# Combined feed-forward weights kept in DRAM after the first token block, and the down projection's differences on VectorE

## The chip, the cores and the metric

The kernel runs on one core of one Trainium2 chip. The metric is the device time of one execution in microseconds (us). The kernel before has a median of 3090.89 us over 3 runs (3089.71 to 3095.99).

## The reference

One layer of a hybrid decoder for 2048 prompt tokens and 32 sample tokens, all in float32. A first half (a gated linear recurrence beside dilated attention) makes `mix`, and then:

```
h  = x + mix @ w_o
hn = rmsnorm(h)
u  = hn @ w_gate                      # 1024 -> 2816
c  = conv_b + sum_j conv_w[j] * u[t - 2 + j]
h  = h + (silu(c) * (hn @ w_up)) @ w_down
h  = h + sigmoid(rmsnorm(h) @ w_ple_gate) * (p @ w_ple_proj)
y  = rmsnorm(h)
```

The change lies in the middle part: the gate, up and down projections.

## The kernel before

Every product of float32 numbers is made of three TensorE passes (`mm3`, L138): each operand is split into a rounded high half and the rest, and high times high, high times rest and rest times high are summed in PSUM. The halves of a weight tile of 128x512 are made by `split_to` (L175): ScalarE copies the raw tile into the high half (L176), VectorE subtracts it from the raw tile to get the rest (L177).

The program has three parts in time. Up to about 1230 us come the input projections, the recurrence and the attention. While the first of the input phases runs, a generator (`down_weights`, L182) makes the down projection's weights on the side: for each of 11 pairs of rows of blocks it loads four quarters, combines and splits them, and stores seven results to a DRAM tile `wd_d`; the loop at L1507 takes two steps of it per step of the phase. Then comes the `trunk` (L936): the tokens are cut into three blocks of 696, 696 and 688, and all blocks pass first through the output projection (`out_block`), then through the feed-forward part (`ffn_block`, L1217), then through the last part (`embed_block`). The feed-forward part of block 0 runs from about 1430 to 1870 us, of block 1 to about 2350 us, of block 2 to about 2810 us.

In the feed-forward part a step `f` (11 in each block) makes 256 of the 2816 columns. A 2x2 product costs seven instead of eight block products (Strassen's scheme in Winograd's form). It needs seven weight operands, numbered 1 to 7 and used in the order 1, 5, 6, 7, 4, 2, 3: numbers 1, 2 and 4 are quarters as they stand in the input; 5, 6, 7 and 3 are sums and differences of quarters. `quarters` (L1135) makes the seven for a gate or an up projection: four loads of 256 KB on SyncE's queue (SP, L942) into the pool of `raw` tiles (7 buffers), then `factors` (L160) with four operations on GpSimd (POOL):

- L164 adds two quarters, when both have landed;
- L166 and L168 subtract;
- L172 overwrites the second scratch tile, so that it waits until VectorE has split what stood there (operand 6).

Each operand is split into a `w` tile, of which there are 6. Before the change this is done anew in each of the three blocks: 66 times in all.

After the up projection, `pair` (L1304) makes the operands of the down projection from the two result tiles `a` and `e`: four differences on POOL (L1315, L1316, L1318, L1319) into two tiles `u`, then ScalarE's copy (L1306) and VectorE's rest (L1307). The `u` tiles are shared with the gate's results of the next step.

The down projection of two steps makes a group (`downs`, L1183). Its seven products are laid between the gate and up products as fourteen halves, one for each entry of `todo`. Its weights are fetched from `wd_d` by DMAs that POOL issues (L1193, 512 KB each, two for each of the seven), into a pool `dw` of 5 buffers: `fetch(x + 2)` is issued when product x starts. POOL works through its instructions in order, and so do SP's queue and ScalarE; the order on each engine is fixed when the program is built, by a scheduler that simulates the program.

Of the kernel before, what the change touches and what calls it, by code (L numbers as in the profile page):

```python
# [11 lines left out]
F32 = mybir.dt.float32  # L12
F32R = mybir.dt.float32r
# [27 lines left out]
USE = (1, 5, 6, 7, 4, 2, 3)  # L41
DOWN_USE = (1, 6, 7, 4, 5, 3, 2)
PAIRS = NF // 2
# [4 lines left out]
def hymba_step_kernel(ctx: ExitStack, tc: tile.TileContext, I: dict, O: dict):  # L48
    nc = tc.nc
    V, A, G, PE, SP = nc.vector, nc.scalar, nc.gpsimd, nc.tensor, nc.sync  # L50

    const = ctx.enter_context(tc.tile_pool(name="const", bufs=1))
    dram = ctx.enter_context(tc.tile_pool(name="scratch", bufs=1, space=DRAM))
# [32 lines left out]
    mix_d = dram.tile([128, NK, NTOK], F32, name="mix_d")  # L86

    wd_d = [dram.tile([7, 128, 2, 512], F32R, name=f"wd{p}_d") for p in range(PAIRS)]
    h_d, hn_d, h2_d = [dram.tile([128, NK, NTOK], F32, name=n) for n in ("h_d", "hn_d", "h2_d")]

    def f32(ap):
        return ap.bitcast(F32)
# [45 lines left out]
    def mm3(ps, wh, wl, xh, xl, first, last, read=False):  # L138

        PE.matmul(ps, lhsT=wh, rhs=xh, start=first, stop=False, skip_group_check=read)  # L140
        PE.matmul(ps, lhsT=wh, rhs=xl, start=False, stop=False, skip_group_check=read)  # L141
        PE.matmul(ps, lhsT=wl, rhs=xh, start=False, stop=last, skip_group_check=read)  # L142
# [14 lines left out]
                lo, hi = 292 * r, 292 * (r + 1)  # L157
                A.dma_start(O[dst][b, lo:hi], I[src][b, lo + 4:hi + 4])

    def factors(a11, a12, a21, a22, tile_, split):  # L160

        yield 1, split(a11)
        s1, s2 = tile_(), tile_()
        G.tensor_add(s1, a21, a22)  # L164
        yield 5, split(s1)
        G.tensor_sub(s2, s1, a11)  # L166
        yield 6, split(s2)
        G.tensor_sub(a21, a11, a21)  # L168
        yield 7, split(a21)
        yield 4, split(a22)  # L170
        yield 2, split(a12)
        G.tensor_sub(s2, a12, s2)  # L172
        yield 3, split(s2)

    def split_to(w, raw):  # L175
        A.copy(w[:, 0], raw)  # L176
        V.tensor_sub(w[:, 1], raw, f32(w[:, 0]))  # L177
        return w
# [3 lines left out]
    def down_weights(pool):  # L182

        tile_ = lambda: pool.tile([128, 512], F32, name="draw", bufs=8)
        for p in range(PAIRS):
            a = [tile_() for _ in range(4)]
            with tc.issue_after(recent[0].ins):
                for x, (i, j) in zip(a, itertools.product(range(2), repeat=2)):
                    SP.dma_start(x, I["w_down"][2 * p + j][:, 512 * i:512 * i + 512])
            for n, w in factors(*a, tile_, lambda raw: split_to(pool.tile([128, 2, 512], F32R, name="dw", bufs=3), raw)):  # L190
                SP.dma_start(f32(wd_d[p][n - 1]), f32(w))
                yield

# [742 lines left out]
    def trunk(cst, rp, ev, sm, tw, hp, sh, wp, dw, pmm, pdn):  # L936
        def raw_tile():
            return rp.tile([128, 512], F32, name="raw")

        def load(src):  # L940
            raw = raw_tile()
            SP.dma_start(raw, src)  # L942
            return raw
# [188 lines left out]
                pair(2, 3, i, xb[i])  # L1132
            yield

        def quarters(src, f):  # L1135

            a = [load(src[f + i][:, 512 * j:512 * j + 512]) for i in range(2) for j in range(2)]
            return dict(factors(*a, raw_tile, split))

        def strassen(w, X, H, put, after, before=lambda n: None):  # L1140

            def product(ps, n, first=True, last=True):
                before(n)
                for k in range(4):
                    kw = slice(128 * k, 128 * k + 128)
                    mm3(ps[:, :H], w[n][:, 0, kw], w[n][:, 1, kw], *X[n][k], first and k == 0, last and k == 3, n not in (2,))
                after(n)

            def copied():
                t = sh.tile([128, 348], F32, name="s")[:, :H]  # L1150
                A.copy(t, pa[:, :H])  # L1151
                return t

            pa, pb, pc = [pmm.tile([128, 512], F32, name="mm") for _ in range(3)]
            product(pa, 1)
            s1 = copied()
            product(pb, 5)
            product(pa, 6, False)
            s2 = copied()
            product(pa, 7, False)  # L1160
            s3 = copied()
            put(1, 1, lambda o, v: V.tensor_add(o, v(pb), v(s3)))
            product(pa, 4, False)
            put(1, 0, lambda o, v: A.copy(o, v(pa)))
            product(pc, 2)
            put(0, 0, lambda o, v: V.tensor_add(o, v(pc), v(s1)))
            product(pb, 3, False)
            put(0, 1, lambda o, v: V.tensor_add(o, v(pb), v(s2)))
# [48 lines left out]
        def ffn_block(b, s, ahead):  # L1217
            t0, T, npr = TRUNK[b]
            H = T // 2
# [4 lines left out]
            for f in range(0, NF, 2):  # L1224
# [36 lines left out]
                def to_u(i, j, put):  # L1261
# [3 lines left out]
                    if n < H:  # L1265
                        put(u[:, npr + 2:npr + 50].rearrange("p (b t) -> p b t", t=6)[:, :, 2:6],
                            lambda t: t[:, n:H].rearrange("p (b t) -> p b t", t=4))

                strassen(quarters(I["w_gate"], f), s.X, H, to_u, after_gate, before)
                gms = []  # L1270
                for i in range(2):
                    u = us[i]
# [19 lines left out]
                def to_gm(i, j, put):  # L1292
# [2 lines left out]
                    cs = slice(H * j, H * j + H)  # L1295
                    V.tensor_mul(gms[i][:, cs], gms[i][:, cs], t)

                strassen(quarters(I["w_up"], f), s.X, H, to_gm, after_up)

                one, two = slice(0, H), slice(H, T)  # L1300
                (a, t), (e, u) = [(g, ev.tile([128, 706], F32, name="u")[:, :T]) for g in gms]
# [2 lines left out]
                def pair(n1, n2, x, n=0):  # L1304
                    hi, lo = wide(T, F32R), wide(T, F32R)
                    copy_after(A.copy(hi, x), n)  # L1306
# [8 lines left out]
                G.tensor_sub(t[:, one], a[:, two], a[:, one])  # L1315
                G.tensor_sub(t[:, two], e[:, two], t[:, one])  # L1316
                pair(5, 6, t, 2 if f < NF - 4 else 0)
                G.tensor_sub(u[:, one], e[:, two], a[:, two])  # L1318
                G.tensor_sub(u[:, two], e[:, one], t[:, two])  # L1319
# [125 lines left out]
        class Block:  # L1445
# [31 lines left out]
    pool = pools(in_st)  # L1477
# [28 lines left out]

    for i, _ in enumerate(in_phase(0, *args, plv, po)):  # L1507
        if i > 8:
            step(down, 2)
    step(down, 1000)  # L1510
    down_st.close()
    pool = pools(hgrn_st, side="right")
    hc, ld, wk, sp = pool("h_c", 1), pool("h_l", 2), pool("h_w", 2), pool("h_s", 2)
    S = []
    for h in range(4):
        s = sp.tile([128, 128], F32, name=f"S{h}")
# [15 lines left out]
    pool = pools(attn_st)  # L1532
# [27 lines left out]
    with ExitStack() as st:  # L1560
        pool = pools(st)
        cp = pool("ffn_c", 1)
        cst = {}
        cst["taps"] = cp.tile([128, NF, 4], F32, name="taps")
        SP.dma_start(cst["taps"], I["taps"])
        cst["conv_s"] = cp.tile([128, NF, 8, 2], F32, name="conv_s")
        SP.dma_start(cst["conv_s"], I["conv_s"])
        cst["halo"] = cp.tile([128, NF, 2], F32, name="halo")
        G.memset(cst["halo"], 0.0)

        tr, tp, dw, ts, th, te, tw, hp = [pool(n, k) for n, k in (
            ("tr", 7), ("tp", 6), ("dw", 5), ("ts", 1), ("th", 6), ("te", 2), ("tw", 44), ("thh", 8))]
# [142 lines left out]
```

## Time and profile before

| | |
|---|---|
| median of 3 runs | 3090.89 us |
| the profiled execution's own time | 3090.4 us |
| its span, first to last instruction | 3088.6 us |
| PE (TensorE matmul) busy | 2952.6 us, 96% |
| DVE (VectorE) busy | 2322.6 us, 75% |
| ACT (ScalarE) busy | 1304.4 us, 42% |
| POOL (GpSimd) busy | 1150.1 us, 37% |
| mean granted TensorE clock | 0.978 |

A group line of the profile has: line, engine, operation, output<-input, shapes, count | busy us, mean ns of one | idle time of the engine before them and what ended it. A line of the waits says which engine and line waited for which, the total in us, how often, and the longest. "L176" is line 176 of the kernel before.

### The profile page before, as it was taken

To read this page: it belongs to the slowest core of one execution; us is meant where nothing else is said; L and a number is where in the kernel's file an instruction comes from. 1 tells how busy PE (TensorE), PEld (TensorE's weight loads), DVE (VectorE), ACT (ScalarE), POOL (GpSimd) and SP (SyncE) were. 2 spreads that over 40 slices of the span, in tenths; PEclk is the share of its full clock that TensorE was granted. 3 is DMA by queue.
4 is the path that set the end of the run, shared out by engine and by line. 5 is a ranking of instruction groups with operands and counts; after the bars stand their busy time and mean duration, and the time that the engine had idled before them with its cause. 6 is when DMAs were issued, how large, how long until landed. Compare 5 with 4: busy or idle time off the path is not lost.

```text
span 3088.6 us, 51939 instructions
## 1 busy us (share of the span) xinstructions
PE 2952.6 (96%) x18639; PEld 2736.8 (89%) x18639; DVE 2322.6 (75%) x4715; ACT 1304.4 (42%) x2824; POOL 1150.1 (37%) x1066
## 2 busy tenths in 40 slices
PE   8999999999889899999999998999999999999998
PEld 8988799987676566998999998999998999999997
DVE  6657757867587687568878678867789878887677
ACT  4332422222266565334444443444444544444443
POOL 1443222222233352003554453545453554543331
PEclk9999999999989999999999999999999999999998
DMA  5899433333438986774556666465667566667453
GB/s 184 321 346 324 144 98 106 110 125 97 134 93 244 261 260 206 252 256 153 176 195 211 206 219 222 160 206 193 211 196 239 185 209 212 205 203 250 139 173 128
DMA packets 296898, 606.38 MB, mean 196 GB/s; under 512 B 42881, under 2 KB 110593, under 8 KB 294849
## 3 DMA queue, kind: packets, MB, share of 16 engines
q1 hardware_dynamic: 259792, 414.96, 41.6%
q0 software_dynamic: 33264, 121.13, 12.3%
q10 hardware_dynamic: 3584, 66.98, 5.9%
q8 instruction: 147, 2.41, 0.3%
q14 instruction: 111, 0.90, 0.1%
HBM read 479.09 MB, written 190.85 MB: 217 GB/s over the span
## 4 chain that ended last, share of the span: by engine, by line
PE 43%; DVE 8%; issue 3%; DMA 3%; POOL 2%; ACT 1%; DVEq 0%; ACTq 0%; POOLq 0%; SPq 0%
PE mm L140 14%; PE mm L142 14%; PE mm L141 14%; DMA w<-wd_d 2%; DVE w L177 2%; DVE h L1209 1%; DVE w L1285 1%; DVE w L1286 1%; POOL raw L164 1%; DVE w L1352 1%; POOL raw L168 0%; ACT w L176 0%; DMA raw<-in_w_up_dram 0%; POOL raw L166 0%; DVE w L1019 0%
## 5 line engine op out<-in xcount | busy, mean ns | idle before, releaser
L141 PE MATMUL mm<-w 128*128 128x348 f32 (+3 forms) x3636 | 1173.7, 323 | 2.2 <-DVE w L1352 1.7
L140 PE MATMUL mm<-w 128*128 128x348 f32 (+3 forms) x3508 | 1114.7, 325 | 52.2 <-DMA w<-wd_d 15.9
L142 PE MATMUL mm<-w 128*128 128x348 f32 (+3 forms) x3508 | 1124.3, 323 | 2.3 <-DVE w L177 2.3
L140 PEld LDWEIGHTS mm<-w 128*128 128x128 f32 x3508 | 662.3, 190 | 63.5 <-DMA w<-wd_d 15.8
L141 PEld LDWEIGHTS mm<-w 128*128 128x128 f32 x3636 | 690.5, 190 | 5.8 <-DVE w L1352 2.6
L142 PEld LDWEIGHTS mm<-w 128*128 128x128 f32 x3508 | 664.4, 190 | 3.7 <-DVE w L177 3.0
L177 DVE TENSOR_TENSOR w<-raw,w 128x512 fp32r<-128x512 f32 x586 | 524.1, 904 | 164.9 <-ACT w L176 159.1
L176 ACT CAST w<-raw 128x512 fp32r<-128x512 f32 x586 | 359.1, 620 | 373.9 <-PE mm L142 267.7
L1209 DVE TENSOR_TENSOR h<-h,mm 128x348 f32<-128x348 f32 (+1 forms) x504 | 243.8, 505 | 47.7 <-PE mm L142 47.0
L164 POOL TENSOR_TENSOR raw<-raw 128x512 f32<-128x512 f32 x66 | 101.3, 1535 | 471.3 <-DMA w<-hn_d 153.0
L1193 POOL DMA_DIRECT2D w<-wd_d x231 | 127.5, 554 | 217.8 <-PE mm L142 192.1
L172 POOL TENSOR_TENSOR raw<-raw 128x512 f32<-128x512 f32 x66 | 96.8, 1467 | 195.2 <-DVE w L177 185.5
L763 ACT ACTIVATE P<-P,st 128x256 f32<-128x256 f32 (+3 forms) x256 | 134.4, 527 | 75.1 <-DVE st L762 70.3
L339 PE MATMUL mm<-wh,xh 128*128 128x512 f32 x352 | 142.0, 405 | 0.0
L341 PE MATMUL mm<-wh,xl 128*128 128x512 f32 x352 | 141.0, 401 | 0.0
L340 PE MATMUL mm<-wl,xh 128*128 128x512 f32 x352 | 140.4, 399 | 0.0
L1000 POOL TENSOR_TENSOR w<-w 128x696 f32<-128x696 f32 (+2 forms) x42 | 74.8, 1789 | 169.2 <-ACT w L999 168.4
L140 PE MATMUL mm<-xh,wh 128*128 128x384 f32 (+2 forms) x384 | 124.7, 330 | 5.5 <-ACT xh L237 5.1
L142 PE MATMUL mm<-xh,wl 128*128 128x384 f32 (+2 forms) x384 | 125.3, 330 | 4.7 <-DVE wl L262 4.5
L762 DVE CUSTOM_DVE_ANT_0 P<-S,mask 128x256 f32<-128x256 f32 (+3 forms) x256 | 106.4, 446 | 27.7 <-PE S L758 18.5
L141 PE MATMUL mm<-xl,wh 128*128 128x384 f32 (+2 forms) x384 | 124.5, 327 | 1.7 <-DVE xl L238 1.7
L1151 ACT COPY s<-mm 128x348 f32<-128x348 f32 (+1 forms) x198 | 87.6, 442 | 79.6 <-PE mm L142 75.6
(352 smaller groups left out, 5656.5 us busy)
## 6 DMA issues: line engine op xcount, KB each, us to landing
w<-wd_d POOLq DMA_DIRECT2D x231, 512.0 KB, 6.0
wd_d<-dw SPq DMA_DIRECT2D x77, 512.0 KB
raw<-in_w_gate_dram SPq DMA_DIRECT2D x132, 256.0 KB
raw<-in_w_up_dram SPq DMA_DIRECT2D x132, 256.0 KB
out_sk_dram<-in_cache_k_dram ACTq DMA_DIRECT2D x56, 584.0 KB
out_sv_dram<-in_cache_v_dram ACTq DMA_DIRECT2D x56, 584.0 KB
wraw<-in_w_in_dram SPq DMA_DIRECT2D x104, 256.0 KB
raw<-in_w_ple_gate_dram SPq DMA_DIRECT2D x64, 256.0 KB
```

The costliest lines, as they stand in the source:

```text
L140: PE.matmul(ps, lhsT=wh, rhs=xh, start=first, stop=False, skip_group_check=read)
L141: PE.matmul(ps, lhsT=wh, rhs=xl, start=False, stop=False, skip_group_check=read)
L142: PE.matmul(ps, lhsT=wl, rhs=xh, start=False, stop=last, skip_group_check=read)
L164: G.tensor_add(s1, a21, a22)
L176: A.copy(w[:, 0], raw)
L177: V.tensor_sub(w[:, 1], raw, f32(w[:, 0]))
L339: PE.matmul(ps, lhsT=xh[k][:, js], rhs=wh, start=k == 0, stop=False)
L340: PE.matmul(ps, lhsT=xh[k][:, js], rhs=wl, start=False, stop=False)
L341: PE.matmul(ps, lhsT=xl[k][:, js], rhs=wh, start=False, stop=k == NK - 1)
L763: A.activation(pe, pe, AF.Exp, bias=mn, scale=-1.0, accum_out=st[:, bl.r, hh, 0:1])
L1193: G.dma_start(t, wd_d[p][n - 1])
L1209: V.tensor_add(o, o, acc[m][:, :H])
```

## The change

1. **Gate and up, block 0.** `factors` hands out raw operands now, and the caller splits them. In block 0 the operands 5, 6, 7 and 3 are, besides, stored from their raw tiles to a new DRAM tile `wg_d`, 256 KB each, by SP: 4 stores for each of 22 sets, 88 in all. The sums on POOL stay.
2. **Gate and up, blocks 1 and 2.** All seven operands are loaded: 1, 2 and 4 from the input, 5, 6, 7 and 3 from `wg_d`. A set has 7 loads in place of 4, and no sums: over both blocks 132 loads more, and 176 operations on POOL fewer.
3. **Down operands.** The four differences of each step move from POOL to VectorE: 132 operations of 128x348 or 128x344.
4. **Room and pace.** The pool `dw` has 6 buffers in place of 5; the room comes from a smaller scratch for the DMAs that POOL issues (`dynamic_dma_scratch_size` 1024 in place of 4096). The generator of the down weights takes 1, 2, 2, 1, 2, 2 ... steps in place of 2 each time.

```diff
-    def factors(a11, a12, a21, a22, tile_, split):
+    COMBINED = (5, 6, 7, 3)
+    def factors(a11, a12, a21, a22, tile_):
-        yield 1, split(a11)
+        yield 1, a11
...
-            for n, w in factors(*a, tile_, lambda raw: split_to(pool.tile([128, 2, 512], F32R, name="dw", bufs=3), raw)):
+            for n, raw in factors(*a, tile_):
+                w = split_to(pool.tile([128, 2, 512], F32R, name="dw", bufs=3), raw)
...
-        def quarters(src, f):
-            a = [load(src[f + i][:, 512 * j:512 * j + 512]) for i in range(2) for j in range(2)]
-            return dict(factors(*a, raw_tile, split))
+        def quarters(name, f, b):
+            part = lambda i, j: load(I[name][f + i][:, 512 * j:512 * j + 512])
+            w = {}
+            if b:
+                for n in USE:
+                    w[n] = split(load(wg_d[name, f // 2][COMBINED.index(n)]) if n in COMBINED else
+                                 part(*{1: (0, 0), 2: (0, 1), 4: (1, 1)}[n]))
+                return w
+            for n, raw in factors(*[part(i, j) for i in range(2) for j in range(2)], raw_tile):
+                if n in COMBINED:
+                    SP.dma_start(wg_d[name, f // 2][COMBINED.index(n)], raw)
+                w[n] = split(raw)
+            return w
...
-                G.tensor_sub(t[:, one], a[:, two], a[:, one])
-                G.tensor_sub(t[:, two], e[:, two], t[:, one])
+                V.tensor_sub(t[:, one], a[:, two], a[:, one])
+                V.tensor_sub(t[:, two], e[:, two], t[:, one])
...
-                G.tensor_sub(u[:, one], e[:, two], a[:, two])
-                G.tensor_sub(u[:, two], e[:, one], t[:, two])
+                V.tensor_sub(u[:, one], e[:, two], a[:, two])
+                V.tensor_sub(u[:, two], e[:, one], t[:, two])
...
-            step(down, 2)
+            step(down, 1 + (i % 3 > 0))
...
-            ("tr", 7), ("tp", 6), ("dw", 5), ("ts", 1), ("th", 6), ("te", 2), ("tw", 44), ("thh", 8))]
+            ("tr", 7), ("tp", 6), ("dw", 6), ("ts", 1), ("th", 6), ("te", 2), ("tw", 44), ("thh", 8))]
...
-    nc = _bacc.Bacc("TRN2", target_bir_lowering=False, num_devices=1, dynamic_dma_scratch_size=4096)
+    nc = _bacc.Bacc("TRN2", target_bir_lowering=False, num_devices=1, dynamic_dma_scratch_size=1024)
```

The order of POOL's instructions, first before the change, in block 1 where the first group of the down projection ends (weights `wd0_d` and `wd1_d`) and the second begins (`wd2_d` and `wd3_d`):

```order
L164 TENSOR_TENSOR raw_21667<-raw_21660,raw_21662 128x512
L1315 TENSOR_TENSOR u_21433<-w_21218 128x348
L1318 TENSOR_TENSOR u_21434<-w_21224,w_21218 128x348
L168 TENSOR_TENSOR raw_21660<-raw_21656,raw_21660 128x512
L166 TENSOR_TENSOR raw_21668<-raw_21667,raw_21656 128x512
L1316 TENSOR_TENSOR u_21433<-w_21224,u_21433 128x348
L1193 DMA w_21413<-wd1_d_86 128x1024
L1193 DMA w_21566<-wd0_d_85 128x1024
L1319 TENSOR_TENSOR u_21434<-w_21224,u_21433 128x348
L172 TENSOR_TENSOR raw_21668<-raw_21658,raw_21668 128x512
L1193 DMA w_21567<-wd1_d_86 128x1024
L1193 DMA w_21881<-wd2_d_87 128x1024
```

The same place after the change, where the fetch of the down weights is at L1208:

```order
L1208 DMA w_21523<-wd1_d_86 128x1024
L1208 DMA w_21676<-wd0_d_85 128x1024
L1208 DMA w_21677<-wd1_d_86 128x1024
L1208 DMA w_21991<-wd2_d_87 128x1024
L1208 DMA w_21992<-wd3_d_88 128x1024
```

In blocks 1 and 2 POOL has nothing left in its row but the fetches. ScalarE's order at the end of block 0, where the last operands of the down projection are copied (L1306) beside the first splits of block 1 (L176), before the change:

```order
L176 CAST w_20192<-raw_20173 128x512
L1312 CAST w_20030<-w_19785 128x348
L176 CAST w_20195<-raw_20169 128x512
L176 CAST w_20199<-raw_20179 128x512
L1151 COPY s_20333<-mm_20202 128x348
L1306 CAST w_20035<-u_20028 128x696
L1306 CAST w_20041<-u_20029 128x696
```

And after it (L176 is L180, L1312 is L1327, L1306 is L1321):

```order
L180 CAST w_20299<-raw_20297 128x512
L1327 CAST w_20140<-w_19891 128x348
L180 CAST w_20304<-raw_20302 128x512
L1321 CAST w_20145<-u_20138 128x696
L1321 CAST w_20151<-u_20139 128x696
L1272 COPY u_20273<-halo_13459 128x2
L1321 CAST w_20155<-w_19897 128x696
L180 CAST w_20309<-raw_20307 128x512
```

The seventh split of the new set stands behind the three copies now; before, it stood ahead of them. Last, SP's order in block 0 after the change, where the sixth gate set is stored and the sixth up set is loaded (`load` is L947, the store L1151):

```order
L1151 DMA w_gate5_d_101<-raw_17511 128x512
L947 DMA raw_17705<-in_w_up_dram 128x512
L1151 DMA w_gate5_d_101<-raw_17519 128x512
L947 DMA raw_17707<-in_w_up_dram 128x512
L947 DMA raw_17709<-in_w_up_dram 128x512
L1151 DMA w_gate5_d_101<-raw_17519 128x512
L947 DMA raw_17711<-in_w_up_dram 128x512
```

Before, these rows held the four loads alone; now the fourth load stands behind the store of operand 3, which waits for POOL's L172 (L176 in the kernel after).

More of the change, by code (lines that the diff above doesn't have):

```diff
@@ L88, in hymba_step_kernel @@
     wd_d = [dram.tile([7, 128, 2, 512], F32R, name=f"wd{p}_d") for p in range(PAIRS)]
+    wg_d = {(n, p): dram.tile([4, 128, 512], F32, name=f"{n}{p}_d") for n in ("w_gate", "w_up") for p in range(PAIRS)}
     h_d, hn_d, h2_d = [dram.tile([128, NK, NTOK], F32, name=n) for n in ("h_d", "hn_d", "h2_d")]
@@ L158, in copy_after @@
                 A.dma_start(O[dst][b, lo:hi], I[src][b, lo + 4:hi + 4])
-    def factors(a11, a12, a21, a22, tile_, split):
-        yield 1, split(a11)
+    COMBINED = (5, 6, 7, 3)
+    def factors(a11, a12, a21, a22, tile_):
+        yield 1, a11
         s1, s2 = tile_(), tile_()
         G.tensor_add(s1, a21, a22)
-        yield 5, split(s1)
+        yield 5, s1
         G.tensor_sub(s2, s1, a11)
-        yield 6, split(s2)
+        yield 6, s2
         G.tensor_sub(a21, a11, a21)
-        yield 7, split(a21)
-        yield 4, split(a22)
-        yield 2, split(a12)
+        yield 7, a21
+        yield 4, a22
+        yield 2, a12
         G.tensor_sub(s2, a12, s2)
-        yield 3, split(s2)
+        yield 3, s2
     def split_to(w, raw):
@@ L1267, in to_u @@
                             lambda t: t[:, n:H].rearrange("p (b t) -> p b t", t=4))
-                strassen(quarters(I["w_gate"], f), s.X, H, to_u, after_gate, before)
+                strassen(quarters("w_gate", f, b), s.X, H, to_u, after_gate, before)
                 gms = []
@@ L1296, in to_gm @@
                     V.tensor_mul(gms[i][:, cs], gms[i][:, cs], t)
-                strassen(quarters(I["w_up"], f), s.X, H, to_gm, after_up)
+                strassen(quarters("w_up", f, b), s.X, H, to_gm, after_up)
                 one, two = slice(0, H), slice(H, T)
```

## The prediction

> **What bounds the kernel now.** I read the page first, then the stages, then what TensorE (PE) waited for.
>
> ```profile
> span 3088.6 us, 51939 instructions
> PE 2952.6 (96%) x18639; PEld 2736.8 (89%) x18639; DVE 2322.6 (75%) x4715; ACT 1304.4 (42%) x2824; POOL 1150.1 (37%) x1066
> ```
>
> PE is the bound. The change leaves its matmuls as they are, so it can only take away or add gaps in PE. The windows show them by stage (us, then busy time of PE, PEld, DVE, ACT, POOL, the clock, the DMA share, GB/s): blocks 0, 1 and 2 of the feed-forward part with the passages between them.
>
> ```profile
> 1440.00:1870.00 430.00, 417.24 (x2579) 414.43 (x2579) 337.89 (x488) 188.80 (x364) 220.91 (x194) 0.99 0.59 195
> 1870.00:1940.00 70.00, 61.53 (x345) 59.77 (x344) 60.94 (x100) 29.37 (x52) 24.46 (x27) 0.90 0.70 225
> 1940.00:2370.00 430.00, 413.26 (x2552) 410.57 (x2551) 340.53 (x502) 184.22 (x359) 207.26 (x194) 0.98 0.60 197
> 2370.00:2450.00 80.00, 74.19 (x463) 72.50 (x463) 70.53 (x110) 42.41 (x93) 41.45 (x31) 1.00 0.66 222
> 2450.00:2780.00 330.00, 330.00 (x2093) 330.00 (x2093) 272.84 (x437) 154.29 (x335) 157.53 (x153) 1.00 0.63 206
> 2780.00:2830.00 50.00, 46.04 (x284) 44.01 (x284) 45.33 (x80) 20.61 (x31) 23.68 (x23) 1.00 0.71 240
> ```
>
> From 1440 to 2830 us PE is idle for 48 us of 1390. In the fifth window it has no gap, at 330 / 2093 = 0.158 us a matmul: that is the floor, and most of the stage runs on it. What ended the gaps of that stage (total, times, longest):
>
> ```profile
> PE mm L140 <- DMA w<-wd_d: 15.9, 6, 5.8
> PE mm L140 <- ACT s L1151: 12.1, 6, 3.4
> PE mm L140 <- DVE w L1122: 4.6, 1, 4.6
> PE mm L140 <- DVE w L1124: 4.6, 1, 4.6
> PE mm L140 <- DVE u L1166: 3.0, 1, 3.0
> ```
>
> These five are 40.2 us. The first is the fetch of down weights, and POOL's timeline ahead of the longest of the six says why it is late:
>
> ```profile
> 2001.86 1.63 POOL L164 TENSOR_TENSOR raw<-raw 128x512 f32<-128x512 f32 x1 [3.25 <-DMA raw<-in_w_up_dram]
> ...
> 2008.29 1.29 POOL L166 TENSOR_TENSOR raw<-raw 128x512 f32<-128x512 f32 x1
> 2009.54 1.40 POOL L1316 TENSOR_TENSOR u<-w,u 128x348 f32<-128x348 f32 x1
> 2010.87 1.11 POOL L1193 DMA_DIRECT2D w<-wd_d  x2
> 2011.98 1.54 POOL L1319 TENSOR_TENSOR u<-w,u 128x348 f32<-128x348 f32 x1
> 2014.76 1.87 POOL L172 TENSOR_TENSOR raw<-raw 128x512 f32<-128x512 f32 x1 [1.23 <-DVE w L177]
> 2016.56 1.11 POOL L1193 DMA_DIRECT2D w<-wd_d  x2
> ```
>
> The fetches stand in POOL's row behind a sum that waits for an up weight to land, and behind the down differences. The chain goes on from there (start, us, what):
>
> ```profile
> 2010.87 12.32 DMA w<-wd_d
> ...
> 2026.50 0.29 PE mm L140
> ...
> 2029.93 0.16 PE mm L141
> ```
>
> The fetch takes 12.32 us, and afterwards PE runs at 0.29 us a matmul before it is back at 0.16. The ten-us windows of two such gaps (same columns):
>
> ```profile
> 1710.00:1720.00 10.00, 7.43 (x29) 7.43 (x30) 1.67 (x3) 1.04 (x3) 1.54 (x2) 0.66 0.67 225
> 2020.00:2030.00 10.00, 6.77 (x25) 6.77 (x26) 0.86 (x1) 0.97 (x2) 1.87 (x2) 0.66 0.69 233
> ```
>
> At 0.16 us, 29 and 25 matmuls are 4.6 and 4.0 us, so the lowered clock costs 2.8 us in each, 5.5 together, on top of the gap.
>
> **The change part by part.** Prices:
>
> ```profile
> L1315 POOL TENSOR_TENSOR u<-w x33: 922/1317/1389, 1467.4 to 2789.2; 128x348 f32<-128x348 f32 x22, 128x344 f32<-128x344 f32 x11
> L1122 DVE TENSOR_TENSOR w<-w x12: 506/509/516, 1403.4 to 2363.8; 128x348 f32<-128x348 f32 x8, 128x344 f32<-128x344 f32 x4
> L172 POOL TENSOR_TENSOR raw<-raw x66: 1257/1490/1925, 1408.7 to 2763.6; 128x512 f32<-128x512 f32 x66
> L177 DVE TENSOR_TENSOR w<-raw,w 128x512 fp32r<-128x512 f32 x586 | 524.1, 904 | 164.9 <-ACT w L176 159.1
> L177 DVE TENSOR_TENSOR w<-raw,w x586: 673/691/3432, 1215.2 to 3067.0; 128x512 fp32r<-128x512 f32 x196
> L1209 DVE TENSOR_TENSOR h<-h,mm x504: 493/504/518, 1502.8 to 2828.8; 128x348 f32<-128x348 f32 x112, 128x344 f32<-128x344 f32 x56
> L1193 POOL DMA_DIRECT2D w<-wd_d x226: 527/541/602, 1473.2 to 2812.0; - x113
> DMA to landing us min/median/max: 3.7/5.9/14.6
> ```
>
> *POOL.* In blocks 1 and 2, 176 sums go, by L172's row 176 x 1.49 = 262 us, and 132 differences, by L1315's 132 x 1.32 = 174 us. None is on PE's path as work; what counts is what stands behind them. In blocks 1 and 2 only fetches are left in POOL's row, so nothing holds them but their buffers.
>
> *The sixth buffer.* A block's 11 steps take 430 us, so one of the seven products of a two-step group comes every 430 / 5.5 / 7 = 11.2 us. With 5 buffers the second tile fetched for product x + 2 takes the place of one that product x reads to its end: a lead of one product, 11.2 us, against landings of 5.9 in the median and 14.6 at most. With 6 both take the places of product x - 1: 22.4 us. So the waits of blocks 1 and 2 should go: of the six, three lie in block 0 (0.5, 3.0 and 2.0 = 5.5 us), three after it (5.8, 3.0, 1.6 = 10.4 us). In block 0 the sums stay ahead of the fetches and I take 3 of 5.5 us. With 4 of the 5.5 us of lowered clock: 10.4 + 3 + 4 = 17.4 us.
>
> *The differences on VectorE.* 132 x 0.51 = 67 us more for DVE, 22 a block. DVE has 430 - 338 = 92 us idle in block 0, which hides them where it isn't late. It is late at the passages, 61 busy of 70 us. There 3 x 4 x 0.51 = 6 us could stand in the path at most, nothing at least; I take 3. On the other side the operands wait less. For the passage 0 to 1, ACT's timeline:
>
> ```profile
> 1868.92 0.62 ACT L176 CAST w<-raw 128x512 fp32r<-128x512 f32 x1 [7.54 <-PE mm L142]
> 1869.45 0.45 ACT L1151 COPY s<-mm 128x348 f32<-128x348 f32 x1
> 1870.12 0.78 ACT L1306 CAST w<-u 128x696 fp32r<-128x696 f32 x1 [0.22 <-POOL u L1316]
> ```
>
> L1306 stood behind a split that waited 7.54 us for PE, and behind POOL's L1316. After the change the split follows it in ACT's order and DVE makes `u` in 2 us. VectorE's L1307 then clears the way for L1122 and L1124 earlier, on which PE waited 4.6 us in each of two passages: I take 6 of 9.2. The u L1166 wait (3.0) came at the end of such a chain through POOL: 2.
>
> *Less contention.* L177 costs 0.904 us in the mean and 0.691 in the median, L1209, with one input in PSUM, never over 0.518. So VectorE's operations with both inputs in SBUF are stretched when POOL works. Blocks 1 and 2 have 2 x 154 splits: 308 x 0.213 = 66 us of DVE come back, more than the 45 us added there. PE's waits on L1151 stand behind the convolution's DVE work in ACT's order; I take 4 of 12.1. The Trainium skill's page "SBUF — State Buffer", section "Who interferes with whom", says that a VectorE instruction with two SBUF inputs contends with a GpSimd instruction that reads SBUF, and that the second to issue blocks until the first is done. That speaks against the change in block 0, where sums stay on POOL: an estimate by it is 88 x 1.49 / 430 = 31% of the time under a sum, 44 moved operations x 0.31 x 0.75 us = 10 us; were all of it on the path, the sum would end at 3074.
>
> *Traffic and SP.* 88 stores are 23 MB in block 0, +54 GB/s on 195; 132 more loads are 17 MB in each later block, +40 GB/s on about 200. The busiest window before:
>
> ```profile
> 110.00:120.00 10.00, 7.75 (x54) 6.73 (x55) 9.50 (x12) 3.04 (x6) 6.66 (x5) 1.00 1.03 400
> ```
>
> At 400 GB/s the engines are full; 250 is below. I take 0; the bounds are 0 and 8 us (half of the fetch waits come back). A load or store costs SP some 0.33 us of issue, hidden. In block 0 a load now stands behind a store that waits for POOL; see the second rival. In blocks 1 and 2 the seven raw buffers let loads run a whole set ahead.
>
> *The pace of the down generator.* It runs at 60 to 300 us, where the window above has 2.25 us of gaps and its neighbour 1.4: a gain of at most 3.7, or as much lost by another order; I take 0. The smaller scratch: nothing in the trace shows a fetch held by it; 0, with 5 us as the bound, a second wait like the longest.
>
> **Sum.** 17.4 + 6 + 2 + 4 - 3 = 26.4 us. The profiled execution took 3090.4 us, the median is 3090.89: 3064.
>
> **The rivals.** *Fetches still late (0.17).* The 12.32 us came with 2.3 MB of cache copies and four weight loads in flight, and there will be more loads. Then the 17.4 us stay and only 6 + 2 + 4 - 3 = 9 are won: 3081. Against it: the lead doubles. The Trainium skill's page "DMA: Bandwidth & Descriptors", section "Queues, rings and completion order", has each DMA engine take its queues in turn, packet by packet, so that every added load slows a fetch; an estimate is 12.3 x 237 / 197 = 14.8 us, which by that rule hides under 22.4 and not under 11.2.
>
> *Block 0 slower (0.10; ends slower).* A raw tile can't be reused until its store has landed, and loads queue behind stores that wait for POOL. If a sum comes late, ACT waits at L176, and the PSUM copy L1151 behind it holds PE. Before:
>
> ```profile
> ACT w L176 <- PE mm L142: 172.4, 133, 9.8
> ACT w L176 <- POOL raw L164: 21.5, 16, 2.9
> ```
>
> ACT already waits 1.3 us at a time for a sum. At 1.5 us more for each of the 22 sets it is 33 us against 26.4 less block 0's 3: 3090 + 33 - 23 = 3100. It decides from 1.1 us a set. Against it: ACT's splits wait eight times as long for PE as for sums, so weights are ahead.
>
> *No change (0.07).* PE waits as long, on another name: 3090.
>
> **How the numbers follow.** The forecast has 0.66. About 0.2%, 6 us, is what a measurement can tell from no change. Faster: forecast and first rival, 0.83, less a little for their edge: 0.82. The same: 0.08. Slower: 0.10. All gaps gone would be 40.2 + 5.5 = 46 us: 3045 is the low end. The high end takes in the first rival with its traffic bound: 3086.
>
> **What would show it.** Right: the wait on wd_d below 4 us in all; L177's mean near 0.7 us in blocks 1 and 2 and still about 0.9 in block 0; POOL busy near 710 us, DVE no more than 2350; the gaps at 1876 and 2340 us shorter. Wrong: the wd_d wait unchanged with longer landings (first rival); new waits of PE on L1151 in block 0 behind ACT's split, with SP waiting on POOL (second); or the stage before 1430 us moved by more than 4 us.

## The result, and the profile after

The changed kernel took 3055.4 us (median of 4 runs, 3049.63 to 3058.33), the kernel before 3092.01 beside it: a ratio of 0.9878, 95% interval 0.986 to 0.9896. It is faster by 36.6 us (1.2%) where 26.4 were forecast, and the time lies inside the range. The ratios below leave out one run in ten of "differences and buffer" at 12659.91 us and two runs of the kernel before at 5724.6 and 3237.04 us, as slow. The profiled execution took 3055.09 us. Its page:

```profile
span 3053.3 us, 52120 instructions
PE 2940.0 (96%) x18639; PEld 2725.0 (89%) x18639; DVE 2247.0 (74%) x4847; ACT 1309.3 (43%) x2824; POOL 740.5 (24%) x758
```

VectorE has 132 instructions more and is busy 75.6 us less. **Where the time went.** Two marks hold the feed-forward stage between them: the first operand pair of block 0 (L1122, now L1127) and the first instruction of the per-layer embedding behind block 2 (L1391, now L1406). Before, then after; the start times are those of the first and the last instruction of the line:

```profile
L1122 DVE TENSOR_TENSOR w<-w x12: 506/509/516, 1403.4 to 2363.8; 128x348 f32<-128x348 f32 x8, 128x344 f32<-128x344 f32 x4
...
L1391 DVE TENSOR_TENSOR w<-mm,w x48: 411/509/608, 2836.9 to 3073.8; 128x348 f32<-128x348 f32 x32, 128x432 f32<-128x432 f32 x8, 128x256 f32<-128x256 f32 x8
```

```profile
L1127 DVE TENSOR_TENSOR w<-w x12: 506/510/515, 1402.8 to 2334.7; 128x348 f32<-128x348 f32 x8, 128x344 f32<-128x344 f32 x4
...
L1406 DVE TENSOR_TENSOR w<-mm,w x48: 416/509/608, 2800.1 to 3038.8; 128x348 f32<-128x348 f32 x32, 128x432 f32<-128x432 f32 x8, 128x256 f32<-128x256 f32 x8
```

From mark to mark it was 2836.9 - 1403.4 = 1433.5 us and is 2800.1 - 1402.8 = 1397.3: 36.2 us less, all of the gain. Below, this is "the stage"; it leaves out what earlier stages add by chance. The same 1310 us of it, before and after (columns as in the prediction):

```profile
1440.00:2750.00 1310.00, 1266.21 (x7833) 1257.26 (x7833) 1061.16 (x1595) 584.40 (x1166) 640.39 (x587) 0.99 0.61 201
```

```profile
1440.00:2750.00 1310.00, 1292.68 (x8067) 1283.73 (x8067) 1013.91 (x1772) 603.48 (x1203) 248.46 (x296) 1.00 0.75 250
```

PE is idle for 26.5 us less. And a matmul takes 1292.68 / 8067 = 160.2 ns, not 1266.21 / 7833 = 161.7: over 7833 of them 11 us. Nearly all of it is the lowered clock after gaps that no longer occur: in the ten-us windows with a granted clock under 0.99 PE is busy 14.0 us longer than its matmuls would take at 0.158 us each before the change, and 4.3 us after it. By block, after:

```profile
1440.00:1870.00 430.00, 419.44 (x2593) 416.65 (x2593) 358.66 (x539) 191.94 (x369) 169.08 (x146) 0.99 0.73 249
1870.00:1940.00 70.00, 68.06 (x414) 65.48 (x413) 61.29 (x111) 35.19 (x65) 6.34 (x12) 1.00 0.86 299
1940.00:2350.00 410.00, 407.75 (x2547) 405.02 (x2546) 301.89 (x552) 181.96 (x350) 40.24 (x76) 1.00 0.75 245
```

The passage from block 0 to 1 carries 414 matmuls in 70 us where it had 345, at a clock of 1.00 in place of 0.90. In block 1 VectorE executes 552 instructions in 302 us; POOL is all but empty. What PE still waits for from 1400 to 2830 us:

```profile
PE mm L142 <- ACT s L1166: 11.5, 13, 2.2
PE mm L142 <- DVE u L1181: 3.2, 1, 3.2
PE mm L143 <- DVE w L1367: 2.7, 4, 1.2
PE mm L142 <- DVE h L1224: 2.0, 7, 0.4
PE mm L142 <- DMA w<-wd_d: 1.7, 4, 0.7
```

The fetches are down from 15.9 to 1.7 us, the two waits of 4.6 in the passages are gone, and the wait on the PSUM copy (12.8 in this stretch before) is nearly as it was. The 3.2 us on L1181 are not new: the gap stands at 1472.7 us, and before the change it stood at 1472.3 with 3.35 us, under the name of the PSUM copy. The split's group (the second figure is its mean in ns), and the landing of the fetches:

```profile
L181 DVE TENSOR_TENSOR w<-raw,w 128x512 fp32r<-128x512 f32 x586 | 436.8, 750 | 193.5 <-ACT w L180 188.2
```

```profile
DMA to landing us min/median/max: 3.7/5.8/13.7
```

SP in block 0 now waits for POOL's sums before it can store them, as the second rival said; ACT's row shows the place where it hurt most, and the chain of waits (third view) what ended it:

```profile
SPq L1151 <- POOL raw L168: 137.1, 20, 9.8
...
SPq L1151 <- POOL raw L176: 59.7, 18, 8.8
```

```profile
1578.60 8.53 ACTq L160 DMA_DIRECT2D out_sk_dram<-in_cache_k_dram  x2
1587.17 0.77 ACT L1321 CAST w<-w 128x696 fp32r<-128x696 f32 x1 [7.80 <-DMA w_up_d<-raw]
...
1588.03 0.44 ACT L1166 COPY s<-mm 128x348 f32<-128x348 f32 x1
```

```profile
1578.16 1.56 POOL raw L168
1579.74 6.85 DMA w_up_d<-raw
1586.61 0.52 ACTq L160
```

ACT issues the copies of the cache. The row of 8.53 us holds two issues (x2): the first starts at 1578.60 us, the second only at 1586.61 and lasts 0.52 us. By its record in the trace the second waits for the semaphore through which SP's store signals that it has landed, and it starts 0.02 us after that signal; the cache copy then signals through the same semaphore. So the wait is one that the program holds: a DMA that takes over a completion semaphore waits until the DMA that had it before has landed, here a store that itself waited for POOL's sum. The PSUM copy stands behind it in ACT's order, and PE loses 2.2 us. In block 0 ACT waited 20.6 us in four such places, and none before the change; the four gaps of PE behind them come to 3.9 us.

### The profile page after: what moved, and what is told of

It reads as the page before. It is cut to its first block, busy times and chain, and to the rows that moved or that the text cites. A ratio compares the mean times of both kernels' runs of the same rounds, so it can differ in the third digit from the quotient of the medians.

```text
span 3053.3 us, 52120 instructions
## 1 busy us (share of the span) xinstructions
PE 2940.0 (96%) x18639; PEld 2725.0 (89%) x18639; DVE 2247.0 (74%) x4847; ACT 1309.3 (43%) x2824; POOL 740.5 (24%) x758
## 4 chain that ended last, share of the span: by engine, by line
PE 47%; DVE 7%; DMA 4%; issue 3%; POOL 1%; ACT 1%; ACTq 0%; SPq 0%; DVEq 0%; POOLq 0%
PE mm L142 14%; PE mm L144 14%; PE mm L143 14%; DVE w L181 1%; DVE h L1224 1%; DMA w_up_d<-raw 1%; DMA raw<-in_w_up_dram 1%; PE acc L787 1%; PE PT L775 1%; POOL raw L168 1%; DMA raw<-in_w_gate_dram 1%; DVE w L1367 1%; DVE w L1301 0%; PE mm L129 0%; PE S L762 0%
## 5 line engine op out<-in xcount | busy, mean ns | idle before, releaser
L142 PE MATMUL mm<-w 128*128 128x348 f32 (+3 forms) x3508 | 1115.2, 324 | 25.3 <-ACT s L1166 11.5
L181 DVE TENSOR_TENSOR w<-raw,w 128x512 fp32r<-128x512 f32 x586 | 436.8, 750 | 193.5 <-ACT w L180 188.2
L180 ACT CAST w<-raw 128x512 fp32r<-128x512 f32 x586 | 360.7, 620 | 414.1 <-PE mm L144 282.8
L1208 POOL DMA_DIRECT2D w<-wd_d x231 | 124.1, 538 | 891.9 <-PE mm L144 764.8
L1166 ACT COPY s<-mm 128x348 f32<-128x348 f32 (+1 forms) x198 | 87.9, 444 | 147.3 <-PE mm L144 147.0
L787 PE MATMUL acc<-pt,v 128*64 128x128 f32 x1136 | 99.9, 294 | 15.1 <-DVE pt L777 12.1
L267 DVE TENSOR_TENSOR wl<-wraw,wh 128x512 fp32r<-128x512 f32 x104 | 87.5, 862 | 26.7 <-POOL wh L148 22.0
```

The source lines that it names most:

```text
L787: PE.matmul(acc[hs, bl.r], lhsT=vals[bl.p, bl.di, c][:, r, hs], rhs=bl.pt[hh][:, i], start=i == 0, stop=i == bl.nk - 1, tile_position=(0, ...
L1208: G.dma_start(t, wd_d[p][n - 1])
```

## The experiments

**The theory.** As in the prediction: down fetches came late because they stood in POOL's row behind sums that wait for weight loads, with a lead of one product; the emptied row and the sixth buffer cure that. **The rivals.** (a) The moved differences are the main cause, by a shorter chain of operands. (b) Contention: POOL's sums slow VectorE's two-input operations down, and that is what they cost, wherever the fetches stand. (c) Each part cures the same waits, so that the parts do not add.

All the results in one place; "stage" is from mark to mark and "fetch" PE's wait on `wd_d` from 1400 to 2830 us, both of the one profiled execution; "split" is the mean of the gate and up split from 1940 to 2350 us (its busy time there by its count).

| kernel | median us | ratio to before, interval | stage us | fetch us | split ns |
|---|---|---|---|---|---|
| before | 3092.0 | | 1433.5 | 15.9 | 949 |
| the change | 3055.4 | 0.9878 (0.986 to 0.9896) | 1397.3 | 1.7 | 683 |
| weights in DRAM only | 3071.3 | 0.995 (0.9927 to 0.9973) | 1404.2 | 11.4 | 736 |
| differences only | 3063.9 | 0.9925 (0.9898 to 0.9953) | 1408.6 | 2.3 | 825 |
| sixth buffer only | 3074.1 | 0.9955 (0.9938 to 0.9972) | 1417.7 | 4.9 | 929 |
| differences and buffer | 3074.7 | 0.9958 (0.9941 to 0.9975) | 1414.3 | 0 | 852 |
| change, 5 buffers | 3049.9 | 0.9876 (0.9847 to 0.9905) | 1395.2 | 4.3 | 682 |
| change, old pace | 3057.5 | 0.9906 (0.9871 to 0.9941) | 1401.1 | 1.6 | 684 |
| useless sums, waiting | 3068.2 | 0.9948 (0.9931 to 0.9965) | 1406.9 | 6.9 | 759 |
| tiny sums, waiting | 3052.4 | 0.9877 (0.9855 to 0.9899) | 1395.6 | 5.8 | 686 |
| useless sums, resident | 3102.3 | 1.0053 (1.0034 to 1.0072) | 1422.3 | 6.2 | 682 |
| sums on VectorE, no DRAM | 3050.7 | 0.987 (0.9846 to 0.9893) | 1391.7 | 1.4 | 683 |
| stores twice | 3069.3 | 0.9934 (0.9909 to 0.9958) | 1417.7 | 1.6 | 686 |
| block 0's sums on VectorE | 3039.7 | 0.9834 (0.9808 to 0.986) | 1381.3 | 0.4 | 684 |

The kernel before was measured again beside each group of runs (medians of 3087.45 to 3092.01 us), and the ratio goes by those. The runs of a kernel spread over 3 to 21 us. The profiled execution of "weights in DRAM only" was the quickest of its six, that of "stores twice" the slowest of its six, that of "block 0's sums" the slowest of its five: there the stage says more, or less, than the median.

**Only the weights in DRAM** (differences on POOL, 5 buffers, old scratch and pace):

```diff
-                V.tensor_sub(t[:, one], a[:, two], a[:, one])
+                G.tensor_sub(t[:, one], a[:, two], a[:, one])
...
-("dw", 6)
+("dw", 5)
```

> The kernel before with only the gate and up weights changed (stored in block 0, loaded in blocks 1 and 2); the down differences stay on POOL, 5 buffers, old scratch, old pace. Theory, that the sums in POOL's row made the fetches late and stretched VectorE: 3065 us (27 won), wait on wd_d below 5 us. Rival, that the sixth buffer took the fetch waits away: 3080 us, wd_d about 12 us. Rival, that the moved differences cleared the passages between blocks: the two waits of PE at 1876 and 2340 us stay at 4 to 5 us each.

It measured 0.995, between the theory and the first rival. PE's waits in the stage:

```profile
PE mm L142 <- ACT s L1166: 14.4, 10, 3.5
PE mm L142 <- DMA w<-wd_d: 11.4, 11, 2.0
PE mm L142 <- DVE h L1224: 3.5, 9, 1.2
```

With every sum gone from POOL's row in blocks 1 and 2, the fetches are still late, in eleven short waits in place of six, the longest 2.0 us in place of 5.8. So the sums ahead of them were not the whole reason: the differences on POOL delay them as well (with the differences gone too, and still 5 buffers, 4.3 us are left). The waits at 1876 and 2340 us are gone although the differences stay on POOL, so the last rival does not hold.

**Only the differences on VectorE**, all four of them:

```diff
-                G.tensor_sub(t[:, one], a[:, two], a[:, one])
+                V.tensor_sub(t[:, one], a[:, two], a[:, one])
```

> The kernel before with only the four down differences moved to VectorE. Theory: the passages get shorter and the fetches stay late: 3083 us (8 won), wd_d still 10 to 16 us. Rival, that the moved differences are the main cause: 3070 us or less. If VectorE at the passages is the limit: 3095.

0.9925: the rival had it right, and the theory, whose 3083 us are 0.9974, was wrong by some 15 us. All sums are still in POOL's row and there are 5 buffers, yet of the waits of before

```profile
PE mm L140 <- ACT s L1151: 16.3, 10, 4.5
...
PE mm L140 <- DMA w<-wd_d: 2.3, 3, 1.1
```

the fetches keep 2.3 us, and L1122 and L1124 no longer appear. The chain of operands got shorter, and POOL does 132 operations fewer beside VectorE; this run does not tell the two apart. Of the chain, in block 0 the operand copy of ACT waited for POOL's second difference before the change (first row), and waits less for VectorE's here (second):

```profile
ACT w L1306 <- POOL u L1316: 46.5, 10, 5.5
```

```profile
ACT w L1306 <- DVE u L1316: 32.2, 11, 6.8
```

**The sixth buffer, taken away or alone.** First the edit of the changed kernel, then that of the kernel before, which gets the smaller scratch as well:

```diff
-("dw", 6)
+("dw", 5)
```

```diff
-("dw", 5)
+("dw", 6)
...
-dynamic_dma_scratch_size=4096
+dynamic_dma_scratch_size=1024
```

> The kernel after with 5 buffers for the down weights. Theory, that a row free of sums is enough: 3058 us (3 lost), wd_d below 5 us. Rival, that the sixth buffer is what hides the fetch: 3070 us, wd_d above 10 us.

> The kernel before with 6 buffers for the down weights and the smaller scratch, nothing else. Theory, that the fetches still stand behind the sums: 3086 us (5 won). Rival, that the buffer count is what matters: 3074 us (the 16 us of waits and part of the slow clock after them), wd_d below 3 us. If the smaller scratch costs: above 3092.

Alone it cuts the fetch wait from 15.9 to 4.9 us and gives 0.9955, so the longer lead does what the prediction's arithmetic says. But without it the changed kernel stands at 0.9876: the other parts have already cured that wait down to 4.3 us.

**The differences and the buffer together** (both edits of the kernel before, as above):

> The kernel before with the differences on VectorE and the sixth buffer and smaller scratch, without weights in DRAM: the sums stay on POOL in all three blocks. Alone the differences gave 0.9925 and the buffer 0.9955. Theory (both cure the same late fetches; after the differences 2.3 us of that wait are left): 0.992, about 3066 us, so that the DRAM weights are worth some 11 us on top. Rival (the gains add): 0.988, 3054 us, and the DRAM weights bring nothing that these two do not.

The fetch wait is gone altogether and the kernel is no faster than with the differences alone: 0.9958 against 0.9925, intervals that touch. Rival (c) holds: the gains do not add. What the DRAM weights bring on top is 0.9958 or 0.9925 against 0.9878, some 15 to 25 us, and no fetch wait is left to explain it. Why the buffer brings nothing here is not shown; each edit also gives every engine a new order of instructions.

**The old pace**, in the changed kernel:

```diff
-            step(down, 1 + (i % 3 > 0))
+            step(down, 2)
```

> The changed kernel with the down generator's old pace (two steps each time). Theory: the pace does nothing, since both kernels stand at the same matmul count at 1440 us (8826 and 8823): the ratio to the kernel before stays that of the change, 0.988, about 3054 us. Rival: the pace bought up to the 3.7 us of gaps of that stage: 0.989, 3057 us or more, and fewer than 8800 matmuls by 1440 us.

0.9906, with an interval that holds the change's 0.9878, and 8806 matmuls by 1440 us against 8823: 17 x 0.155 = 2.6 us (1367 us busy by 8823). By this count the pace brings 0 to 3 us; the ratios alone are too wide to say so.

**Contention or waiting?** Two kernels put the work back on POOL without the need for it. Both are the changed kernel with 5 buffers (0.9876); for each combined weight that blocks 1 and 2 load, POOL adds it to itself, all 512 columns or only 8:

```diff
+                    if n in COMBINED:
+                        G.tensor_add(idle, raw, raw)
```

```diff
+                    if n in COMBINED:
+                        G.tensor_add(idle, raw[:, :8], raw[:, :8])
```

> The changed kernel with 5 buffers; in blocks 1 and 2 POOL also makes one useless sum from each of the four combined tiles that are loaded, with a result that nobody reads. So POOL again stands waiting for weight loads and again works beside VectorE, while the weights still come ready from DRAM. The same kernel without these sums was 0.9876 of the kernel before; moving the differences alone, with all sums kept, was 0.9925. Theory (POOL's sums cost that difference, by their waits or by contention): 0.992, about 3066 us, with the split's mean near 0.8 us. Rival (what counts is that a combined weight needs one landing in place of two to four): 0.988, 3054 us, although the split's mean is 0.8 us.

> As the run with useless sums that wait for loaded tiles, at the same places of POOL's row, but each adds only 8 columns in place of 512: POOL waits for the same weight loads with the fetches behind it, and hardly works beside VectorE. That run gave 0.9948, and the same kernel without useless sums 0.9876. If the sums cost by their waits in POOL's row: 0.994, about 3069 us. If they cost by the work beside VectorE (contention): 0.988, about 3051 us, with the split's mean near 0.74 us as without the sums.

The added line L1149 on POOL (min, median, max in ns), and what POOL sat idle for ahead of it (us, times), with 512 columns and then with 8:

```profile
L1149 POOL TENSOR_TENSOR idle<-raw x176: 1029/1058/4086, 1833.3 to 2733.1; 128x512 f32<-128x512 f32 x176
...
  DMA raw<-w_gate_d: 210.4, 64
  DMA raw<-w_up_d: 199.0, 63
```

```profile
L1149 POOL TENSOR_TENSOR idle<-raw x176: 187/199/1118, 1827.5 to 2713.9; 128x8 f32<-128x8 f32 x176
...
  DMA raw<-w_gate_d: 260.1, 84
  DMA raw<-w_up_d: 207.3, 75
```

The second kernel's POOL stands waiting for loads for 467 us, more than the first's 409, with all fetches behind it, and costs nothing: 0.9877, and a stage of 1395.6 us against 1395.2 without any such sums. The first, with 176 x 0.86 = 151 us more of POOL's work at the medians, is at 0.9948, and its stage is 11.3 us longer. By the ratios the difference is some 22 us. So it is the work beside VectorE that costs, not the waiting in the row. Nor do the longer sums hold back loads by the raw tiles that they read: from 1870 to 2830 us SP's loads wait for VectorE's split in both kernels alike (677.6 and 672.2 us) and for POOL's sums not at all and 0.6 us. What grows is ACT's wait for VectorE's convolution (L1305), from 14.8 us with the tiny sums to 35.4. This is rival (b), and the forecast had put 4 us on it. For PE it appears as no wait of its own: the same waits (PSUM copy 13.1 against 9.9, `h` 4.8 against 3.3, fetches 6.9 against 5.8) all get a little longer; VectorE stands behind the first two. The Trainium skill's page "SBUF — State Buffer", section "Who interferes with whom", calls the port pair that VectorE and GpSimd share an exclusive lock; the split at 759 ns with the full sums and 686 with the tiny ones agrees.

**The same sums on a resident tile**, meant to separate the same two:

```diff
-                        G.tensor_add(idle, raw, raw)
+                        G.tensor_add(idle, idle, idle)
```

> As the run with useless sums from the loaded tiles, but each useless sum works in place on a tile that stays in SBUF, so that it waits for no load: POOL works as long beside VectorE, but nothing in its row waits. If contention with VectorE is what the sums cost: 0.992, about 3066 us, as there. If it is their waits for loads, with fetches behind them: 0.988, 3054 us, with the split's mean near 0.8 us all the same. If both runs stand at 0.988, POOL's sums cost nothing once the differences are gone from its row.

It failed as that test: since they wait for nothing, all 176 ran early, between 1213.7 and 1537.2 us, and none beside blocks 1 and 2. It shows contention with POOL far busier, ahead of and at the start of the stage, whose mark (L1127) comes at 1426.8 us in place of 1395.5. 1440 to 1540 us with them, and in the changed kernel with 5 buffers:

```profile
1440.00:1540.00 100.00, 68.47 (x343) 62.93 (x344) 95.24 (x101) 40.60 (x74) 75.19 (x52) 0.81 0.39 135
```

```profile
1440.00:1540.00 100.00, 93.81 (x567) 92.72 (x566) 88.43 (x124) 49.87 (x96) 42.80 (x31) 0.97 0.67 227
```

With POOL busy for 75% of the time VectorE's mean instruction takes 95.24 / 101 = 943 ns in place of 713; it becomes the bound, and PE is busy 27% less in that stretch, at a clock a sixth lower. The two windows lie at different distances from the mark, so this is an upper figure: from 1470 to 1570 us, as far from the mark as the second window, it is 888 ns, 82.49 us of PE and a clock of 0.91.

**Is the DRAM needed?** The kernel before with the differences and all sums on VectorE, 6 buffers, and nothing in DRAM:

```diff
-            return dict(factors(*a, raw_tile, split))
+            return dict(factors(*a, raw_tile, split, V))
```

> The kernel before with the differences and all gate and up sums on VectorE, the sixth buffer and the smaller scratch, and no weights in DRAM: POOL's row holds only fetches in all three blocks, as after the change in blocks 1 and 2, without its stores and added loads. If what the DRAM weights bring is an empty POOL row: 0.988 as the change, about 3051 us. Rival (VectorE's row now waits for loads, and has 264 sums of some 0.6 us more, 53 us a block): 0.995 or more, 3072 us, with new waits of PE on VectorE's operations.

0.987, as the change, without its 58 MB of traffic. POOL's row holds only fetches, VectorE does 264 sums more, and of the feared waits on VectorE's row few come: 3.1 us of PE on L1168, while its wait on the PSUM copy falls to 4.2 us, from 11.5 in the changed kernel. VectorE from 1940 to 2350 us:

```profile
1940.00:2350.00 410.00, 407.32 (x2539) 403.61 (x2538) 343.72 (x630) 182.20 (x352) 40.22 (x76) 1.00 0.67 218
```

630 instructions in 344 us, 546 ns each; in the prediction's row of that block 502 took 341, 678 ns each.

**The stores' price**: block 0's 88 stores made twice, the second into a tile of DRAM that nothing reads:

```diff
-                    SP.dma_start(wg_d[name, f // 2][COMBINED.index(n)], raw)
+                    for d in (wg_d, wx_d):
+                        SP.dma_start(d[name, f // 2][COMBINED.index(n)], raw)
```

> The changed kernel with each of block 0's 88 stores made twice, the second into a tile of DRAM that nothing reads: 23 MB more in block 0, and each raw tile is held until both have landed. Theory (the stores are hidden, as the prediction had it at 0): within 0.2% of the change, 0.988, about 3051 us, the extra traffic seen in the first window only. Rival (stores hold raw tiles and the loads queued behind them): block 0 gets longer by 5 us or more, 0.990 or more, with more waits of PE on L1166 there.

0.9934 against 0.9878, some 17 us slower than the change: the rival. Its largest gap in block 0, in the chain of waits (start, us, what):

```profile
1629.89 8.71 DMA raw<-in_w_gate_dram
1638.62 0.52 ACTq L161
1639.23 0.14 ACT w L1323
...
1640.19 0.35 ACT s L1168
...
1640.59 0.66 PE mm L143
```

It is the pattern of the changed kernel: the second of two cache copies waits for the semaphore of a transfer of SP, here a load that took 8.71 us, and the PSUM copy behind it holds PE. Three such copies are issued at 1638.62, 1724.32 and 1808.44 us, and the gaps of PE that end 2 us after them are 9.7, 3.4 and 2.1 us: 15.2 together, 11 more than in the changed kernel, of a stage that is 20.4 us longer. In the ten us from 1630 PE executes 6 matmuls, and the DMA share is 0.98.

**Block 0's sums on VectorE too** (the changed kernel, with the engine of `factors` made a parameter):

```diff
-            for n, raw in factors(*[part(i, j) for i in range(2) for j in range(2)], raw_tile):
+            for n, raw in factors(*[part(i, j) for i in range(2) for j in range(2)], raw_tile, V):
```

> The changed kernel with the sums of block 0 on VectorE too (the down weights' sums of the early stage stay on POOL). Theory (POOL's sums in block 0 delay splits and stores; VectorE's two-input operations get faster without them): the waits on L1166 and u L1181 in block 0, 10 us together, go by half: 0.986, about 3048 us. Rival (VectorE, 359 us busy of 430 in block 0, gets 88 sums of some 0.6 us more and holds the products): slower than the change by 10 to 20 us, 0.992.

3039.66 us, 0.9834: the best of all, some 14 us (0.44%) ahead of the change by the ratios; the theory had it right, and PE is idle for 3.2 us of block 0 in place of 10.6. Block 0 (columns as above):

```profile
1440.00:1870.00 430.00, 426.77 (x2667) 424.23 (x2666) 357.17 (x642) 196.21 (x374) 37.66 (x71) 1.00 0.77 257
```

Its sum L168, here on VectorE, and in the changed kernel on POOL, with that of the early down weights:

```profile
L168 DVE TENSOR_TENSOR raw<-raw x22: 679/692/694, 1397.2 to 1810.8; 128x512 f32<-128x512 f32 x22
```

```profile
L168 POOL TENSOR_TENSOR raw<-raw x22: 1292/1700/5586, 1392.0 to 1820.1; 128x512 f32<-128x512 f32 x22
L168 POOL TENSOR_TENSOR draw<-draw x11: 1282/1288/1299, 79.7 to 287.6; 128x512 f32<-128x512 f32 x11
```

VectorE does 103 instructions more in block 0 and is busy 1.5 us less. ACT's waits on SP's stores (20.6 us) are gone with them, though the 88 stores are still made; their sums take 0.69 us in place of 1.70. Beside "sums on VectorE, no DRAM", which also leaves POOL only fetches, it has a stage 10.4 us shorter, and its median is 11.0 us lower: that is what the combined weights in DRAM are worth by themselves, for 176 sums x 0.69 = 121 us of VectorE.

## Why the prediction was right, and where it was not

Right are the sign, the place (all gain lies in the feed-forward stage) and the size: 3055.4 us for 3064. That the sum comes so near is in part luck, for 17.4 of its 26.4 us rest on a lead that the change turned out not to need, and what it gained by contention and the clock was put too low. Term by term:

- **Fetch waits, 13.4 forecast, 14.2 measured** (15.9 to 1.7). The size is right; the reason is not. "The fetches stand in POOL's row behind a sum that waits for an up weight to land" was read from the row, but a row with 467 us of such waits costs nothing (tiny sums), and moving the differences alone leaves 2.3 us. The lead argument holds where the buffer is the only change (4.9 left), but the change does not need the buffer.
- **The lowered clock, 4 forecast, 11 measured.** This is the term that was mis-sized most. I had counted it at the two longest fetch gaps, 5.7 us by the ten-us windows; the passages held another 6.7 us (the clock went from 0.90 to 1.00 in one of them).
- **The passages, 6 forecast, 9.2 measured**: both waits on L1122 and L1124 went. Neither appears in any of the three kernels with one part alone, not even with the buffer alone, so any one part, or the new order of instructions that comes with it, is enough to clear them (with the buffer alone 2.2 us appear on L1307 in their place). The wait of 3.0 on L1166 (2 forecast), at 2413 us, went too.
- **Contention, 4 forecast.** I looked for it in the waits on the PSUM copy, which fell from 12.8 to 11.5 us, and not at all once two gaps near 1472 and 1491 us that changed their names are counted in both (14.7 and 14.7): two gaps of 3.2 and 2.5 us at 1925 and 1959 us shrank, and 3.9 us came in block 0. It works through all of VectorE's chain: 151 us of POOL's work put back in blocks 1 and 2 cost 11.3 us of the stage. The step that failed is "66 us of DVE come back", treated as cover and not as time on the path.
- **The differences' cost, 3 forecast**: only L1367 waits 1.0 us longer. The Trainium skill's rule, taken to its end, gave 3074 by 10 us lost in block 0; that loss did not come (VectorE's splits there went from 137.0 to 129.1 us for 150), probably because the differences left POOL as well. Its direction is right: with POOL empty in block 0 the stage is 16.0 us shorter still.
- **Traffic, 0 forecast.** Landings stayed (6.0 to 5.8 us in the median, 14.6 to 13.7 at most), so the first rival fell; an estimate of 14.8 us, after the Trainium skill's page "DMA: Bandwidth & Descriptors", section "Queues, rings and completion order", was not reached. The stores are not free, though: 88 more of them cost some 17 us. The second rival's mechanism is there (SP waits 137 us for L168) but it cost PE 3.9 us, not 33, and by another path than the late splits that the rival named: four cache copies of ACT waited for the semaphores of late stores.

What "would show it" came out so: the fetch wait below 4 (1.7), L181 at 683 ns in block 1 but 860 (129.05 / 150) in block 0, POOL at 740 where 710 was named, DVE 2247, and the passages' gaps closed.

**Open.** What the first 88 stores cost besides the 3.9 us behind held cache copies is not known; a kernel with these copies issued elsewhere was not tried. It is open, too, how the gain of the moved differences divides between a shorter chain and less contention. Every edit makes the scheduler order all engines anew, and no run holds that order fixed. The runs of one kernel differ by 0.1 to 0.7%, and each kernel has one profile, so that the split of the last 10 us between clock, contention and chance is the profiles' word only.

## What to carry to other kernels

Work that is put on an idle engine is not free if that engine slows the busy one: price it by the busy engine's stretched means (median against mean in one row shows it) and test it by putting useless work back. Before believing that a queue's order is the cause, put a tiny operation with the same waits in the same places. And when several edits cure one wait, run each alone: here three parts of 0.45 to 0.75% made 1.2% together, one of them needless. Last, a DMA that a compute engine issues can hold up that engine's own work, here by a completion semaphore that another queue's late transfer still had.

## What was not expected of the hardware

- A sum of 128x512 takes POOL 1.29 us in the early stage and 1.70 in the median in block 0; VectorE does it in 0.69, and its split, at 684 ns with POOL empty, takes 860 to 950 beside POOL's work. So VectorE was busy no longer in block 0 when it did all of POOL's sums itself.
- A POOL that only waits does VectorE no harm: with 467 us of waits ahead of tiny sums the split is at 686 ns, and at 759 with full sums behind the same loads.
